# One 512-column product in place of two 256-column products in the down projections of a streaming-encoder block

## The chip, the core and the metric

The kernel runs on one core of one Trainium2 chip. The metric is the device time of one execution in microseconds (us), lower being better. A core has TensorE (in the rows PE for the products and PEld for the loads of their weights), VectorE (DVE), ScalarE (ACT), GpSimd (POOL) and SyncE (SP, which issues the transfers from HBM). SBUF is the on-chip memory; PSUM holds what TensorE writes, in banks of 512 fp32 values for each of 128 partitions.

## What is computed

One layer on 256 tokens of width 2048: a SwiGLU block, a mixer (a causal convolution group beside a gated DeltaNet group), a second SwiGLU block, each with an adaLN modulation that comes from `c`.

```
mods = (silu(c) @ w_ada + b_ada).reshape(B, 9, 2048)
h = modulate(rmsnorm(x, ffn1_norm), mods[:, 0], mods[:, 1])
x = x + 0.5 * mods[:, 2] * ((silu(h @ wg) * (h @ wu)) @ wd)     # wd: 5632 x 2048
h = modulate(rmsnorm(x, mix_norm), mods[:, 3], mods[:, 4])
x = x + mods[:, 5] * (concat(conv_group(h @ w_in), deltanet_group(h @ w_in)) @ w_out)
h = modulate(rmsnorm(x, ffn2_norm), mods[:, 6], mods[:, 7])
x = x + 0.5 * mods[:, 8] * ((silu(h @ wg2) * (h @ wu2)) @ wd2)
out = rmsnorm(x, final_norm)
```

The change is in the two products with `wd` and `wd2`, the down projections.

## The kernel before

Activations lie transposed: features on partitions, the 256 tokens (`T`) along the free dimension. A weight matrix is cut into 128x128 tiles; each is the stationary operand of a product, and the activations stream past it as 256 columns.

**Split products.** A weight in fp32 is split into two fp32r parts: ACT copies it to `hi` (L122), DVE subtracts to get `lo` (L124); one such step handles half a 1 MB load, that is eight tiles. Activations are kept as two parts too, side by side in one tile `act` of shape [128, 2, 256]: part 0 is the high part `rhi`, part 1 the low part `rlo`. A tile's product is three fp32r products into the same 256 columns of a bank (`mm3`, L151 to L153): whi by rhi, whi by rlo, wlo by rhi. Three buffers each for `hi` and `lo` and four for the raw loads limit how far ACT, DVE and the loads run ahead.

**The stages.** In `ffn` the 44 inner tiles (5632 rows) are taken in two halves of 22 (`FH`). For a half, the up and gate projections come first (`col_pair`, L368; activations are split by L298 and L299), then the down projection: for each of 16 output tiles `m`, 22 tiles of `wd` against the 22 `act` tiles, accumulated in one bank, after which DVE's `residual` (L315) adds gate times bank to x. So there are four stretches of down projection, called here the first, second (block one), third and fourth (block two), of 352 tiles each. In the second and fourth, each x tile is then squared for the next norm (L186 on ACT, L182 on DVE), and in the second also made into the mixer's input (`h_pre`, L264 to L268).

**Beside it.** In block one DVE also reduces the modulation weights `w_ada` in the background (`ada`, L218, 2.3 us each with its own 1 MB load), at a fixed number per weight step. In the mixer DVE runs 240 convolution taps (L552), GpSimd runs the small chains of inverse square roots (L166 to L169, each started by DVE's L160 and L162), and TensorE carries `w_in`, the DeltaNet products and `w_out`. The output product `w_out` takes the DeltaNet half first (most of it in plain fp32, L906) and the convolution half last; L830 transposes the DeltaNet output for it.

**What sets the order.** A scheduler orders the instructions of each engine with its own estimate of their times, along the priorities of program order. An edit in one stage can thus reorder instructions in later ones. Each engine then runs its list strictly in order.

Of the kernel before, what the change touches and what calls it, by code (L numbers as in the profile page):

```python
# [16 lines left out]
T = 256  # L17
# [4 lines left out]
FH = FT // 2  # L22
# [31 lines left out]
class Body:  # L54
# [93 lines left out]
    def mm3(self, out, whi, wlo, rhs, start, stop):  # L148
        nc = self.nc
        rhi, rlo = rhs  # L150
        nc.tensor.matmul(out, lhsT=whi, rhs=rhi, start=start, stop=False)  # L151
        nc.tensor.matmul(out, lhsT=whi, rhs=rlo, start=False, stop=False)  # L152
        nc.tensor.matmul(out, lhsT=wlo, rhs=rhi, start=False, stop=stop)  # L153

    def rsqrt(self, v, n, tag, pool=None, beside=False):

        nc = self.nc
        y = self.tile(pool or self.small, [P, n], tag + "y")
        t = self.tile(self.small, [P, n], tag + "t")
        nc.vector.tensor_scalar(out=t.bitcast(I32), in0=v.bitcast(I32), scalar1=1, scalar2=None,  # L160
                                op0=ALU.logical_shift_right)
        self.seed = nc.vector.tensor_scalar(out=y.bitcast(I32), in0=t.bitcast(I32), scalar1=-1.0, scalar2=1597463007.0,  # L162
                                            op0=ALU.mult, op1=ALU.add)
        for _ in range(3):
            if beside:
                nc.gpsimd.tensor_tensor(out=t, in0=y, in1=y, op=ALU.mult)  # L166
                nc.gpsimd.tensor_tensor(out=t, in0=t, in1=v, op=ALU.mult)
                nc.gpsimd.tensor_scalar(out=t, in0=t, scalar1=-0.5, scalar2=1.5, op0=ALU.mult, op1=ALU.add)
                nc.gpsimd.tensor_tensor(out=y, in0=y, in1=t, op=ALU.mult)  # L169
                continue  # L170
            nc.vector.scalar_tensor_tensor(out=t, in0=y, scalar=-0.5, in1=y, op0=ALU.mult, op1=ALU.mult)
            nc.vector.tensor_tensor(out=t, in0=t, in1=v, op=ALU.mult)
            nc.vector.scalar_tensor_tensor(out=y, in0=t, scalar=1.5, in1=y, op0=ALU.add, op1=ALU.mult)
        return y
# [152 lines left out]
    def ffn(self, which, gate, done, after):  # L327
        gu, wd, f0 = self.gu_d[which], self.wd_d[which], len(done)
        for half in range(2):
            acts = list(done) if half == 0 else []  # L330
            for f in range(half * FH + len(acts), (half + 1) * FH):
                ps = [self.bank(self.spare if f == f0 else None)[:, 0:T] for _ in range(2)]
                self.col_pair(ps, gu[f - f0])
                acts.append(self.ffn_evac(*ps))
            n = 0
            for ch in range(FH):
                for hi, lo in self.weights(wd[half, ch]):
                    for k in range(8):
                        m, j = divmod(n, FH)
                        if j == 0:  # L340
                            ps = self.bank()
                        self.mm3(ps[:, 0:T], hi[:, k, :], lo[:, k, :], self.rhs(acts[j]), j == 0, j == FH - 1)
                        if j == FH - 1:
                            while not half and self.ready < gate * 16 + m:
                                next(self.bg[0])
                            self.residual(m, ps[:, 0:T], gate)
                            if half:
                                self.squares(m)
                                after(m)
                        n += 1  # L350
# [668 lines left out]
```

## Time and profile before

| | |
|---|---|
| runs | 1944.02 us median of 3 (1943.39 to 1948.23) |
| the profiled execution | 1943.16 us, of which the span of its instructions is 1941.1 us |
| TensorE products busy | 1894.9 us, 98% of the span, 16206 products |
| DVE busy | 1493.6 us, 77% |
| ACT busy | 916.1 us, 47% |
| DMA | 503.63 MB, mean 259 GB/s |

A busy TensorE is not one at its peak, since its products overlap; how fast it goes is read from the distance between the starts of two products.

### The profile page before, as it was taken

The numbers are of one execution on the slowest core, as the hardware profiler recorded it, in microseconds if no ns is written. First come the engines' busy times: TensorE is split into PE (matmuls) and PEld (weight loads), VectorE is DVE, ScalarE is ACT, GpSimd is POOL, SyncE is SP. The second block draws the span as 40 slices with busy tenths as digits, with TensorE's granted clock in tenths as the row PEclk, the third lists the DMA queues.
The fourth block names the chain that finished last, engine by engine and source line by source line (L and its number), as shares of the span: only waits on it lengthen the run. The fifth ranks groups of instructions, "written<-read, shape, count | busy, mean of one in ns | idle before, by whom it ended". The sixth has DMA issues, their size and how long they took to land.

```text
span 1941.1 us, 38412 instructions
## 1 busy us (share of the span) xinstructions
PE 1894.9 (98%) x16206; PEld 1873.8 (97%) x16206; DVE 1493.6 (77%) x2191; ACT 916.1 (47%) x1298; POOL 96.8 (5%) x195
## 2 busy tenths in 40 slices
PE   5999999999999999999999899999999999999997
PEld 4999999999999999999999889999999999999997
DVE  6989898888878899889999888867775455555554
ACT  3454553344444445754546436544443344444453
POOL 1000000000000000070022300000000000000000
PEclk9999999999999999999999999999999999999999
DMA  8998788899989897457664265567776555555552
GB/s 322 388 361 357 266 338 337 347 349 349 359 350 361 325 350 312 176 182 273 241 207 153 87 240 196 194 238 280 298 278 213 194 194 195 195 195 196 196 195 87
DMA packets 71087, 503.63 MB, mean 259 GB/s; under 512 B 8321, under 2 KB 8961, under 8 KB 10497
## 3 DMA queue, kind: packets, MB, share of 16 engines
q1 hardware_dynamic: 69554, 499.60, 67.9%
q8 instruction: 127, 2.08, 0.4%
q0 software_dynamic: 1360, 1.58, 0.3%
q14 instruction: 46, 0.38, 0.1%
HBM read 498.52 MB, written 2.62 MB: 258 GB/s over the span
## 4 chain that ended last, share of the span: by engine, by line
PE 89%; DVE 5%; POOL 2%; ACT 2%; DMA 1%; issue 1%; DVEq 0%; SPq 0%; ACTq 0%; POOLq 0%
PE ps L368 36%; PE ps L153 16%; PE ps L152 16%; PE ps L151 16%; PE ps L906 2%; DVE lo L124 1%; DMA raw<-in_wa 1%; PE ps L684 1%; DVE raw L218 1%; DVE cva L552 1%; POOL dt L520 1%; ACT hi L122 1%; DVE kq L246 0%; DMA raw<-in_w_ada 0%; DMA x<-in_x 0%
## 5 line engine op out<-in xcount | busy, mean ns | idle before, releaser
L122 ACT ACTIVATE hi<-raw 128x1024 fp32r<-128x1024 f32 x643 | 681.8, 1061 | 893.0 <-PE ps L152 423.8
L124 DVE TENSOR_TENSOR lo<-raw,hi 128x1024 fp32r<-128x1024 f32 x643 | 786.5, 1225 | 371.0 <-ACT hi L122 369.6
L368 PE MATMUL ps<-h,hi 128*128 128x256 f32 x4160 | 640.7, 276 | 0.0
L368 PEld LDWEIGHTS ps<-h,hi 128*128 128x128 f32 x4160 | 548.9, 188 | 0.0
L152 PE MATMUL ps<-h,hi 128*128 128x256 f32 (+1 forms) x1664 | 459.3, 281 | 3.2 <-DVE h L249 3.2
L151 PE MATMUL ps<-h,hi 128*128 128x256 f32 (+1 forms) x1664 | 454.1, 280 | 7.2 <-ACT hi L122 3.9
L153 PE MATMUL ps<-h,lo 128*128 128x256 f32 (+1 forms) x1664 | 439.8, 280 | 0.3 <-DVE lo L124 0.2
L368 PE MATMUL ps<-h,lo 128*128 128x256 f32 x2080 | 404.8, 276 | 0.0
L151 PE MATMUL ps<-act,hi 128*128 128x256 f32 x1408 | 387.1, 276 | 1.0 <-ACT hi L122 1.0
L152 PE MATMUL ps<-act,hi 128*128 128x256 f32 x1408 | 387.5, 276 | 0.0
L153 PE MATMUL ps<-act,lo 128*128 128x256 f32 x1408 | 386.4, 276 | 0.8 <-DVE lo L124 0.8
L218 DVE CUSTOM_DVE_ANT_0 raw<-raw,cb 128x2048 f32<-128x2048 f32 x144 | 329.5, 2290 | 6.6 <-DMA raw<-in_w_ada 6.3
L151 PEld LDWEIGHTS ps<-h,hi 128*128 128x128 f32 x1664 | 311.4, 189 | 9.2 <-ACT h L248 4.4
L152 PEld LDWEIGHTS ps<-h,hi 128*128 128x128 f32 x1664 | 312.9, 188 | 5.0 <-DVE h L249 3.7
L368 PEld LDWEIGHTS ps<-h,lo 128*128 128x128 f32 x2080 | 313.2, 188 | 0.0
L153 PEld LDWEIGHTS ps<-h,lo 128*128 128x128 f32 x1664 | 302.6, 189 | 2.4 <-DVE lo L124 1.1
L151 PEld LDWEIGHTS ps<-act,hi 128*128 128x128 f32 x1408 | 264.0, 188 | 1.4 <-ACT hi L122 1.4
L153 PEld LDWEIGHTS ps<-act,lo 128*128 128x128 f32 x1408 | 263.3, 188 | 1.2 <-DVE lo L124 1.2
L152 PEld LDWEIGHTS ps<-act,hi 128*128 128x128 f32 x1408 | 264.0, 188 | 0.0
L552 DVE SCALAR_TENSOR_TENSOR cva<-xz,prm,cva 128x251 f32<-128x251 f32 (+15 forms) x240 | 105.3, 483 | 1.2 <-ACT cva L548 0.7
L315 DVE SCALAR_TENSOR_TENSOR x<-ps,mods,x 128x256 f32<-128x256 f32 x96 | 46.2, 482 | 27.1 <-PE ps L153 26.5
L906 PE MATMUL ps<-xz,raw 128*128 128x256 f32 x224 | 50.9, 386 | 0.3 <-DVE x L315 0.3
(238 smaller groups left out, 921.1 us busy)
## 6 DMA issues: line engine op xcount, KB each, us to landing
raw<-in_w_ada SPq DMA_DIRECT2D x144, 1024.0 KB, 6.5
raw<-in_gu SPq DMA_DIRECT2D x130, 1024.0 KB, 4.9
raw<-in_wd SPq DMA_DIRECT2D x88, 1024.0 KB, 4.9
raw<-in_w_in SPq DMA_DIRECT2D x42, 1024.0 KB, 5.0
raw<-in_wa SPq DMA_DIRECT2D x40, 1024.0 KB, 8.5
raw<-in_w_out SPq DMA_DIRECT2D x16, 1024.0 KB, 4.8
raw<-in_wk SPq DMA_DIRECT2D x6, 1024.0 KB, 6.5
raw<-in_gw SPq DMA_DIRECT2D x6, 1024.0 KB, 4.7
```

Of the source, the lines that this page charges most:

```text
L122: nc.scalar.activation(out=hi, in_=raw, func=AF.Copy)
L124: nc.vector.tensor_tensor(out=lo, in0=raw, in1=hi.bitcast(F32), op=ALU.subtract)
L151: nc.tensor.matmul(out, lhsT=whi, rhs=rhi, start=start, stop=False)
L152: nc.tensor.matmul(out, lhsT=whi, rhs=rlo, start=False, stop=False)
L153: nc.tensor.matmul(out, lhsT=wlo, rhs=rhi, start=False, stop=stop)
L218: nc.vector.tensor_tensor_reduce(out=w, in0=w, in1=self.cb, scale=1.0, scalar=0.0, op0=ALU.mult, op1=ALU.add, accum_out=self.macc[:, n:n + 1])
L315: self.nc.vector.scalar_tensor_tensor(out=xm, in0=ps, scalar=self.mods[:, gate * 16 + m:gate * 16 + m + 1], in1=xm, op0=ALU.mult, op1=ALU.add)
L368: nc.tensor.matmul(ps[g], lhsT=w[:, 2 * k + g, :], rhs=r, start=start, stop=stop)
L520: nc.gpsimd.tensor_scalar(out=gs[:, i, :], in0=self.low, scalar1=g2[:, b * 4 + i:b * 4 + i + 1], scalar2=None, op0=ALU.mult)
L552: self.taps[j] = nc.vector.scalar_tensor_tensor(out=acc[:, i:T], in0=xs[:, 0:T - i], scalar=w(TAPS - 1 - i), in1=acc[:, i:T], op0=ALU.mult ...
L684: nc.tensor.matmul(ps[:, i * P:(i + 1) * P], lhsT=lhs[:, i, :], rhs=rhs[:, i, :], start=True, stop=True)
L906: nc.tensor.matmul(ps, lhsT=w[:, k, :], rhs=self.zs[k], start=k == 0, stop=k == 7)
```

## The change

`mm3` gives way to `mm2` in the down projections alone. One product of whi now streams both activation parts, 512 columns, into a whole bank: its first half collects whi by rhi, its second whi by rlo. wlo by rhi, 256 columns, goes on top of the second half. `residual` then adds the two halves of the bank to x one after the other, which is one DVE instruction more for each `m`, 64 in all. TensorE has 1408 products fewer and as many columns as before.

```
+    def mm2(self, bank, whi, wlo, rhs, start, stop):
+
+
+        nc = self.nc
+        nc.tensor.matmul(bank, lhsT=whi, rhs=rhs, start=start, stop=False)
+        nc.tensor.matmul(bank[:, 1, :], lhsT=wlo, rhs=rhs[:, 0, :], start=False, stop=stop)
...
                         if j == 0:
-                            ps = self.bank()
-                        self.mm3(ps[:, 0:T], hi[:, k, :], lo[:, k, :], self.rhs(acts[j]), j == 0, j == FH - 1)
+                            ps = self.bank().rearrange("p (g t) -> p g t", g=2)
+                        self.mm2(ps, hi[:, k, :], lo[:, k, :], acts[j], j == 0, j == FH - 1)
                         if j == FH - 1:
                             while not half and self.ready < gate * 16 + m:
                                 next(self.bg[0])
-                            self.residual(m, ps[:, 0:T], gate)
+                            for g in range(2):
+                                self.residual(m, ps[:, g, :], gate)
```

The lines of everything below the new function move by seven or eight: L315 becomes L322, L218 L225, L552 L560, L160 L167, L162 L169, L207 L214.

TensorE at the end of the fourth stretch, before: three products for each tile of `wd`.

```order
L151 MATMUL ps_22782<-act_21366,hi_22831 128x256
L152 MATMUL ps_22782<-act_21366,hi_22831 128x256
L153 MATMUL ps_22782<-act_21366,lo_22833 128x256
L151 MATMUL ps_22782<-act_21490,hi_22831 128x256
L152 MATMUL ps_22782<-act_21490,hi_22831 128x256
L153 MATMUL ps_22782<-act_21490,lo_22833 128x256
```

The same place in the change, two tiles' products and the sum over tokens that follows:

```order
L159 MATMUL ps_21459<-act_20358,hi_21494 128x512
L160 MATMUL ps_21459<-act_20358,lo_21496 128x256
L159 MATMUL ps_21459<-act_20482,hi_21494 128x512
L160 MATMUL ps_21459<-act_20482,lo_21496 128x256
L202 MATMUL ps_21519<-col,acc_20548 128x1 x2
```

A tile costs two products in place of three; what follows is in the same order.

DVE in the mixer, before, at the DeltaNet's output norm: `rqy` starts the chain of the query norm on GpSimd, and `ot`, which reads what that chain leaves in `osc`, starts the next. Between them stood 17 rows; these are the last of them.

```order
L552 SCALAR_TENSOR_TENSOR cva_11373<-xz_11371,prm,cva_11373 128x255
L124 TENSOR_TENSOR lo_13438<-raw_13434,hi_13436 128x1024
L552 SCALAR_TENSOR_TENSOR cva_11216<-xz_11214,prm,cva_11216 128x254
L218 ISA raw_13680,macc<-raw_13680,cb 128x2048
L218 ISA macc 128x1
L552 SCALAR_TENSOR_TENSOR cva_11373<-xz_11371,prm,cva_11373 128x254
L160 TENSOR_SCALAR ot_12877<-osc_12872 128x8
```

The same place in the change, from `rqy` to `ot`:

```order
L169 TENSOR_SCALAR rqy_12112<-rqt_12113 128x16
L784 SCALAR_TENSOR_TENSOR R_11411<-ps_12244,nbk_9279,R_11411 128x128 x2
L560 SCALAR_TENSOR_TENSOR cva_10233<-xz_10231,prm,cva_10233 128x232
L560 SCALAR_TENSOR_TENSOR cva_10390<-xz_10388,prm,cva_10390 128x232
L124 TENSOR_TENSOR lo_12669<-raw_12637,hi_12667 128x1024
L560 SCALAR_TENSOR_TENSOR cva_10233<-xz_10231,prm,cva_10233 128x231
L560 SCALAR_TENSOR_TENSOR cva_10390<-xz_10388,prm,cva_10390 128x231
L124 TENSOR_TENSOR lo_12705<-raw_12701,hi_12703 128x1024
L560 SCALAR_TENSOR_TENSOR cva_10233<-xz_10231,prm,cva_10233 128x230
L560 SCALAR_TENSOR_TENSOR cva_10390<-xz_10388,prm,cva_10390 128x230
L167 TENSOR_SCALAR ot_12205<-osc_12200 128x8
```

The scheduler has moved `ot` up: it now follows `rqy` after ten instructions, not 17 rows, and the weight remainders (L124) that TensorE needs next stand behind it.

TensorE in the mixer, in the change, around the product that spreads the convolution group's norm over the partitions (L214, before L207). `h_12854` to `h_12871` are the DeltaNet half of `w_out`'s input, `h_12958` is the first tile of the convolution half, which comes out of that norm.

```order
L214 MATMUL ps_12952<-ht_12949,ones 128x256
L153 MATMUL ps_13170<-h_12854,lo_13168 128x256
L151 MATMUL ps_13170<-h_12858,hi_13166 128x256
L152 MATMUL ps_13170<-h_12858,hi_13166 128x256
L153 MATMUL ps_13170<-h_12858,lo_13168 128x256
L151 MATMUL ps_13170<-h_12867,hi_13166 128x256
L152 MATMUL ps_13170<-h_12867,hi_13166 128x256
L153 MATMUL ps_13170<-h_12867,lo_13168 128x256
L151 MATMUL ps_13170<-h_12871,hi_13166 128x256
L152 MATMUL ps_13170<-h_12871,hi_13166 128x256
L153 MATMUL ps_13170<-h_12871,lo_13168 128x256
L151 MATMUL ps_13210<-h_12958,hi_13206 128x256
```

Ten products now stand between the norm's product and the first that needs the normed tile; before it was followed by 13 plain products of L906 and 48 split ones. SP's list is the same row for row.

## Rows read from the trace of the kernel before

**Rows 1.** The page: span, busy engines, the chain that ended last.

```profile
span 1941.1 us, 38412 instructions
...
PE 1894.9 (98%) x16206; PEld 1873.8 (97%) x16206; DVE 1493.6 (77%) x2191; ACT 916.1 (47%) x1298; POOL 96.8 (5%) x195
...
PE 89%; DVE 5%; POOL 2%; ACT 2%; DMA 1%; issue 1%; DVEq 0%; SPq 0%; ACTq 0%; POOLq 0%
```

**Rows 2.** Busy time by stretch: the four down projections in order.

```profile
core 0: us, PE busy (x) PEld busy (x) DVE busy (x) ACT busy (x) POOL busy (x), PEclk, DMA share, GB/s
282.60:404.00 121.40, 119.60 (x1036) 118.72 (x1035) 101.63 (x121) 47.10 (x48) 0.00 (x0) 1.00 0.88 343
644.00:763.00 119.00, 119.00 (x1052) 119.00 (x1051) 109.90 (x159) 59.38 (x91) 0.00 (x0) 1.00 0.90 355
1448.50:1567.50 119.00, 119.00 (x1052) 119.00 (x1052) 63.04 (x65) 46.87 (x46) 0.00 (x0) 1.00 0.57 206
1807.50:1926.50 119.00, 119.00 (x1053) 119.00 (x1052) 63.17 (x73) 57.56 (x74) 0.00 (x0) 1.00 0.45 160
```

**Rows 3.** Timeline of TensorE's products in the third stretch: start, duration, line.

```profile
1500.00 0.28 PE L153 MATMUL ps<-act,lo 128*128 128x256 f32 x1
1500.11 0.28 PE L151 MATMUL ps<-act,hi 128*128 128x256 f32 x1
1500.23 0.28 PE L152 MATMUL ps<-act,hi 128*128 128x256 f32 x1
1500.34 0.28 PE L153 MATMUL ps<-act,lo 128*128 128x256 f32 x1
```

**Rows 4.** Plain fp32 products: two merged timeline rows, and durations (min/median/max ns).

```profile
1130.38 11.82 PE L906 MATMUL ps<-xz,raw 128*128 128x256 f32 x54
...
L906 PE MATMUL ps<-xz,raw x224: 379/379/796, 1104.0 to 1156.1; 128*128 128x256 f32 x112
...
1074.69 0.95 PE L606 MATMUL ps<-ones,ht 128*128 128x1 f32 x8
...
L606 PE MATMUL ps<-ones,ht x64: 164/250/250, 818.6 to 1075.4; 128*128 128x1 f32 x64
```

**Rows 5.** Busy time in a stretch of 258-column split products.

```profile
1212.00:1236.00 24.00, 24.00 (x199) 23.95 (x199) 20.09 (x44) 13.64 (x22) 0.00 (x0) 1.00 0.48 176
```

**Rows 6.** DVE's groups in the second stretch, and two adjacent residual adds.

```profile
L124 DVE TENSOR_TENSOR lo<-raw,hi 128x1024 fp32r<-128x1024 f32 x44 | 53.8, 1223 | 7.3 <-ACT hi L122 7.2
...
L315 DVE SCALAR_TENSOR_TENSOR x<-ps,mods,x 128x256 f32<-128x256 f32 x15 | 7.2, 481 | 1.8 <-PE ps L153 1.8
...
300.08 0.88 DVE L315 SCALAR_TENSOR_TENSOR x<-ps,mods,x 128x256 f32<-128x256 f32 x2 [2.39 <-PE ps L153]
```

**Rows 7.** Waits in the first stretch: total us, times, longest.

```profile
PEld ps L151 <- ACT hi L122: 1.4, 2, 0.8
PEld ps L153 <- DVE lo L124: 1.2, 2, 0.7
```

**Rows 8.** Busy time at the end of the second stretch, with the transfer rate.

```profile
744.00:763.00 19.00, 19.00 (x170) 19.00 (x169) 17.89 (x27) 9.16 (x13) 0.00 (x0) 1.00 0.98 404
```

**Rows 9.** Timeline: the last residual add of the fourth stretch.

```profile
1927.02 0.48 DVE L315 SCALAR_TENSOR_TENSOR x<-ps,mods,x 128x256 f32<-128x256 f32 x1 [5.53 <-PE ps L153]
```

**Rows 10.** Timeline of the mixer's end on DVE, PE and ACT, and the taps' group.

```profile
1079.83 0.18 DVE L162 TENSOR_SCALAR rqy<-rqt 128x16 int32<-128x16 int32 x1
...
1090.60 0.17 DVE L160 TENSOR_SCALAR ot<-osc 128x8 int32<-128x8 int32 x1 [1.23 <-POOL osc L812]
...
L552 DVE SCALAR_TENSOR_TENSOR cva<-xz,prm,cva 128x251 f32<-128x251 f32 (+15 forms) x240 | 105.3, 483 | 1.2 <-ACT cva L548 0.7
...
1101.35 2.71 PE L830 MATMUL ps<-ident,A 128*128 128x128 f32 x8 [5.57 <-ACT A L818]
...
1150.25 0.59 PE L207 MATMUL ps<-ht,ones 128*128 128x256 f32 x2
...
1154.62 0.41 ACT L298 ACTIVATE h<-cva 128x256 fp32r<-128x256 f32 x1
```

## The prediction, made before the changed kernel had run

> **What bounds the kernel now.** I read the page first: TensorE's products cover 98% of the span, and 89% of the chain that ended last is TensorE [rows 1]. But busy says little of products that overlap, so the next view is busy time by stretch, cut at the four down projections [rows 2]. In the second, third and fourth, TensorE is never idle and holds 1052 or 1053 products in 119.0 us, at a granted clock of 1.00, which is 2.4 GHz. Less the one still running at the cut that is 119.0 / 1051 = 0.1132 us from start to start, and single rows of the timeline show the same 0.11 or 0.12 us steps without a gap [rows 3]. These three stretches are bound by how fast TensorE takes one product after another; DVE is busy for 53% of the third and fourth, and 92% of the second [rows 2]. The first stretch is slightly different: 1036 products at 0.1132 us would take 117.3 of its 121.4 us, so 4.1 us go to waits, and these are for the split of weights: 1.4 us for ACT's `hi` and 1.2 us for DVE's `lo` among them [rows 7]. So what the change is worth is the time of one tile of `wd`, three steps of 0.1132, 339.7 ns, times 1408 tiles, less what DVE does to it.
>
> **What a product's 113.2 ns is made of.** 256 columns at 2.4 GHz and one cycle each would be 106.7 ns. The 6.5 ns above that decide this case. The nearest rows are the plain fp32 products. Those of L906, 256 columns each, stand 54 in 11.82 us; less the last one's own 379 ns that is 11.44 / 53 = 215.9 ns from start to start [rows 4], or 512 cycles (213.3 ns) and 2.6. So a product that occupies the array for 512 cycles has a surplus of 2.6 ns, not 13. And products of one single column still take (0.95 - 0.25) / 7 = 0.10 us on average [rows 4], though their column is nothing. Each carries a 128x128 weight load, and I take that load as the floor: with 256 columns the array's 107 to 109 ns are a little shorter than the load behind it, with 512 cycles the load is hidden. A wide fp32r product then takes what L906 takes, 215.9 ns, and the narrow one that follows keeps 113.2, since the next tile's whi is loaded behind it.
>
> **The sum.** A tile costs 215.9 + 113.2 = 329.1 ns in place of 339.7. 10.6 ns by 352 tiles is 3.7 us for each stretch, 14.9 us for four. The bounds of this term: if the 6.5 ns belong to every product whatever its length, the wide one takes 219.8 and a tile gains 6.7 ns, 9.4 us in all; if the narrow product too escapes the floor behind a wide one (109.3), a tile gains 14.5 ns, 20.4 us. If the surplus belongs to the columns, nothing is gained (a rival, below). I take 14.9, because L906 has the cycles of the wide product and the same weight load.
>
> The Trainium skill, page "TensorE: Matmul & The Clock Gate", section "Wait — 56ns, not 53.3ns?", has start to start as N / 2.4 GHz and about 2.5 ns. L906's 215.9 ns agrees with it, the 113.2 ns of the split products do not (it would have 109.2). By the page alone a tile goes from 327.6 to 325.0 ns, an estimate, and the change would give 3.6 us.
>
> **DVE** gets 64 instructions, 16 in each stretch. Two adjacent residual adds take 0.88 us, the second starting 0.40 us after the first [rows 6], so 6.4 us more DVE work in each stretch. In the third and fourth DVE has 63 of 119 us of work, and the second add hides in that room; without that cover it would be 0.40 us a time, 6.4 us a stretch. The bank it holds longer is one of four, each filled for 22 tiles (7.2 us), so TensorE does not wait for it.
>
> In the second stretch there is little room: 109.9 + 6.4 = 116.3 us of work against 352 x 0.3291 = 115.8 us of TensorE. DVE also waits there 7.2 us for ACT's `hi` and 1.8 us for residuals [rows 6]. Behind a waiting residual stand the next `lo` remainders, which TensorE needs. The loss lies between 0 (DVE's lead of up to two weight steps covers the 0.5 us it lacks, and the waits for `hi` shrink as DVE falls behind) and 116.3 + 9.0 - 115.8 = 9.5 us (every wait stays). I take 1.5, near the low end, as a late engine no longer waits.
>
> In the first stretch DVE has 101.6 + 6.4 = 108.0 us of work for 117.7 us, enough on average. At its start, where the split is what TensorE waits for [rows 7], one more residual goes ahead of the next remainder, 0.4 us, and the following ones a little later: 1.0 us, between 0 and 6.4.
>
> **Transfers.** SP's list is unchanged. The first two stretches move 343 and 355 GB/s [rows 2]; 3% faster they ask for 353 and 366, and 404 GB/s are reached in the last 19 us of the second [rows 8]. I cost it at nothing.
>
> **The end.** The last residual starts at 1927.02 us with nothing behind it but the norm and the store [rows 9]; a second add there costs its 0.4 us in full.
>
> **The mixer** is not edited, but its order is. Before, TensorE waited 5.57 us for the DeltaNet output (L830) [rows 10]. In the changed order the query-norm chain is started earlier against TensorE's work and the first head group's chain runs alone on GpSimd, so most of this wait should go: up to 5.6 us gained. Two things give it back. `ot` waits for GpSimd's `osc`, which takes 1090.60 - 1080.01 = 10.6 us after `rqy` [rows 10]; in between DVE now has two remainders at 1.22, six taps at 105.3 / 240 = 0.44 and two short adds, some 5.5 us in all, so it stands still for about 5 us with the next remainder behind it, and TensorE, about two steps (5.4 us) of weights ahead, then loses perhaps 2 to 3. And the convolution norm's product now has ten products (1.1 us) between it and the first that needs the normed tile; before, that tile's high part ended 1155.0 - 1150.25 = 4.8 us after the product [rows 10]. So about 3 us of wait appear there. These cancel; I count zero, and from a gain of 5.6 to a loss of 6 for the range.
>
> Together: -14.9 + 1.5 + 1.0 + 0.4 + 0 = -12.0 us. The profiled execution took 1943.2 us (its span and 2.1 us around it), 0.9 us below the median of the runs shown; from 1943.2 I get 1931.2, and as a median 1932.
>
> **The rivals.**
>
> *The columns set the pace.* The change has as many columns as before. If the split products' 6.5 ns come with the columns (a stream slowed by 6%), the wide product takes 2 x 113.2 = 226.4 ns, a tile 339.6, and nothing is gained; DVE's 2.9 us remain: 1944.0 + 2.9 = 1947, no change. For it: the two kinds of product differ only in type, and only the split ones show the 6.5 ns. Against it: the 0.10 us of one-column products. By the rule of the Trainium skill's page above, an estimate again, 3.6 us less 2.9 would be gained, 1943, which is no change either.
>
> *DVE and the mixer take the gain.* If in the second stretch half of the 9.5 us is lost and the mixer loses 4, the sum is -14.9 + 4.8 + 1.0 + 0.4 + 4 = -4.7: 1939, no change. For it: 92% busy DVE in strict order. Against it: block two alone, with DVE half idle, gives 7.5.
>
> *The wide stream meets the weight loads* and ends on the other side. Split products with 258 columns, whose parts lie two columns further in their tiles, start 199 in 24.0 us, 24.0 / 198 = 121.2 ns apart [rows 5], 8 ns more than 256 columns for two more, so the place in SBUF from which a stream is read can cost time. The wide product reads part 0 and part 1 in one stream. If it is slowed as these are over its whole length, it takes 242 ns and a tile 242.4 + 121.2 = 363.6, 23.9 ns more than now: 1408 x 0.0239 = 33.7 us, 1944 + 33.7 + 2.9 = 1981. It decides from a tile above 339.7 - 2.0 + 4.1 = 342 ns, a wide product of 229. Against it: the tiles do not move, and the parts already are read from these places at 113.2.
>
> *Both escape the floor*: 325.2 ns a tile, -20.4 + 2.9 = -17.5, 1926.
>
> **The numbers.** The forecast 0.59, both escape 0.10, columns 0.12, DVE and mixer 0.11, wide stream slower 0.08. I hold 0.3% (5.8 us) to be about what a measurement of this kernel tells from no change. Faster: 0.59 + 0.10 and 0.01 of the DVE case, 0.70; same 0.22; slower 0.08. The range runs from 1923 (20.4 gained, nothing lost) to 1943 (the mixer's loss of 6 and the low end of the pair, 9.4, with DVE at 3); it leaves out the slow stream and most of the columns' case.
>
> **What the profile would show.** Wide products 216 ns before the next start and narrow ones 113, four stretches of 116 us (the first 119 to 120), 1408 products fewer. Wrong: a wide product of 220 or more; TensorE waiting for `lo` in the second stretch by more than 2 us; the wait at L830 still there, or waits around the convolution norm beyond 6 us.

## The result: slower by 1.1%, in the products that were to gain

The changed kernel takes 1969.08 us (median of 4, 1965.71 to 1973.51), the kernel before 1946.12 us beside it (median of 4, 1943.39 to 1954.66). The ratio is 1.0112, with a 95% interval of 1.0073 to 1.015. The forecast was 1932, with a range up to 1943: wrong in sign, since the wide product takes 229 or 236 ns where 215.9 had been put in.

The page of the changed kernel, against [rows 1]: fewer products, and yet more time of TensorE.

```profile
span 1967.1 us, 35638 instructions
...
PE 1913.7 (97%) x14798; PEld 1826.4 (93%) x14798; DVE 1519.2 (77%) x2255; ACT 918.4 (47%) x1301; POOL 107.9 (5%) x195
...
PE 88%; DVE 5%; DMA 3%; POOL 2%; issue 1%; ACT 1%; SPq 0%; DVEq 0%; ACTq 0%; POOLq 0%
```

Busy time by stretch, the four down projections, against [rows 2] (same columns):

```profile
283.80:410.40 126.60, 124.27 (x705) 107.12 (x704) 109.35 (x141) 48.50 (x51) 0.00 (x0) 1.00 0.87 337
649.80:772.80 123.00, 123.00 (x705) 107.33 (x705) 115.17 (x173) 59.71 (x91) 0.00 (x0) 1.00 0.90 344
1464.10:1588.00 123.90, 123.90 (x705) 107.03 (x704) 70.01 (x80) 47.23 (x46) 0.00 (x0) 1.00 0.57 198
1827.60:1951.60 124.00, 124.00 (x705) 107.16 (x705) 70.01 (x88) 57.80 (x74) 0.00 (x0) 1.00 0.44 153
```

The reader is to see three things. TensorE is busy without a hole in the last three stretches, so nothing that it waits for explains them. The granted clock is 1.00 as before. And the last two stretches, in which DVE has over 50 us to spare, are the longest: 704 products in 123.9 us are 352 ns for a pair, against the 339.7 of three narrow products and the 329.1 of the forecast. The second add did double its work in the second stretch (L322, 30 adds, against 15 in [rows 6]), and DVE found the room:

```profile
L322 DVE SCALAR_TENSOR_TENSOR x<-ps,mods,x 128x256 f32<-128x256 f32 x30 | 14.4, 480 | 2.2 <-PE ps L160 2.2
```

The timeline of TensorE in the fourth stretch, against [rows 3]: start, duration, line.

```profile
1859.87 0.40 PE L159 MATMUL ps<-act,hi 128*128 128x512 f32 x1
1860.10 0.28 PE L160 MATMUL ps<-act,lo 128*128 128x256 f32 x1
1860.22 0.40 PE L159 MATMUL ps<-act,hi 128*128 128x512 f32 x1
1860.45 0.28 PE L160 MATMUL ps<-act,lo 128*128 128x256 f32 x1
1860.57 0.40 PE L159 MATMUL ps<-act,hi 128*128 128x512 f32 x1
```

Two pairs in 0.70 us, 350 ns each at this resolution. The trace holds the starts in ns, and most pairs fall into two kinds: 229 ns for the wide product, or 236, each with 117 or 118 for the narrow one, so about 347 or 353 ns a tile. One kind holds for many tiles on end: in the third and fourth stretches nearly all tiles of the first two banks take 347, those of the other fourteen 353.

Where the 26.0 us between the two profiled spans lie, from the first to the last start of each stretch: the four stretches themselves 3.0, 3.4, 4.4 and 4.4 us, together 15.2; the way from the second to the third (the mixer and block two's first up projection; the up projections between the other stretches take 239.5 us in both) 6.3; the time before the first stretch 3.3; the tail 1.0. The 3.3 are not the change's: TensorE's list is the same row for row up to there, and over the sixteen profiles of this case the first down product starts between 277.4 and 282.5 us.

### The profile page after: what moved, and what is told of

It reads as the page before. It is cut to its first block, busy times and chain, and to the rows that moved or that the text cites. A ratio compares the mean times of both kernels' runs of the same rounds, so it can differ in the third digit from the quotient of the medians.

```text
span 1967.1 us, 35638 instructions
## 1 busy us (share of the span) xinstructions
PE 1913.7 (97%) x14798; PEld 1826.4 (93%) x14798; DVE 1519.2 (77%) x2255; ACT 918.4 (47%) x1301; POOL 107.9 (5%) x195
## 4 chain that ended last, share of the span: by engine, by line
PE 88%; DVE 5%; DMA 3%; POOL 2%; issue 1%; ACT 1%; SPq 0%; DVEq 0%; ACTq 0%; POOLq 0%
PE ps L376 36%; PE ps L159 16%; PE ps L160 8%; PE ps L153 8%; PE ps L152 8%; PE ps L151 8%; PE ps L914 2%; DMA raw<-in_w_ada 2%; DVE lo L124 1%; DVE cva L560 1%; PE ps L692 1%; DVE raw L225 1%; DMA raw<-in_wa 0%; DMA ls<-scr_l 0%; DVE kq L253 0%
## 5 line engine op out<-in xcount | busy, mean ns | idle before, releaser
L124 DVE TENSOR_TENSOR lo<-raw,hi 128x1024 fp32r<-128x1024 f32 x643 | 786.0, 1224 | 352.3 <-ACT hi L122 351.4
L159 PE MATMUL ps<-act,hi 128*128 128x512 f32 x1408 | 492.6, 395 | 0.8 <-ACT hi L122 0.8
L160 PE MATMUL ps<-act,lo 128*128 128x256 f32 x1408 | 387.4, 279 | 1.6 <-DVE lo L124 1.6
L225 DVE CUSTOM_DVE_ANT_0 raw<-raw,cb 128x2048 f32<-128x2048 f32 x144 | 329.0, 2286 | 8.8 <-DMA raw<-in_w_ada 8.6
L159 PEld LDWEIGHTS ps<-act,hi 128*128 128x128 f32 x1408 | 261.6, 187 | 63.2 <-ACT hi L122 1.4
L160 PEld LDWEIGHTS ps<-act,lo 128*128 128x128 f32 x1408 | 263.7, 187 | 5.6 <-DVE lo L124 2.8
L560 DVE SCALAR_TENSOR_TENSOR cva<-xz,prm,cva 128x251 f32<-128x251 f32 (+21 forms) x240 | 105.3, 480 | 6.0 <-DMA ls<-scr_l 5.6
L322 DVE SCALAR_TENSOR_TENSOR x<-ps,mods,x 128x256 f32<-128x256 f32 x160 | 76.7, 481 | 38.1 <-PE ps L160 29.3
L914 PEld LDWEIGHTS ps<-xz,raw 128*128 128x128 f32 x224 | 42.3, 190 | 6.4 <-DVE xz L842 0.8
```

The lines of the kernel that those rows point to most:

```text
L124: nc.vector.tensor_tensor(out=lo, in0=raw, in1=hi.bitcast(F32), op=ALU.subtract)
L159: nc.tensor.matmul(bank, lhsT=whi, rhs=rhs, start=start, stop=False)
L160: nc.tensor.matmul(bank[:, 1, :], lhsT=wlo, rhs=rhs[:, 0, :], start=False, stop=stop)
L225: nc.vector.tensor_tensor_reduce(out=w, in0=w, in1=self.cb, scale=1.0, scalar=0.0, op0=ALU.mult, op1=ALU.add, accum_out=self.macc[:, n:n + 1])
L322: self.nc.vector.scalar_tensor_tensor(out=xm, in0=ps, scalar=self.mods[:, gate * 16 + m:gate * 16 + m + 1], in1=xm, op0=ALU.mult, op1=ALU.add)
L560: self.taps[j] = nc.vector.scalar_tensor_tensor(out=acc[:, i:T], in0=xs[:, 0:T - i], scalar=w(TAPS - 1 - i), in1=acc[:, i:T], op0=ALU.mult ...
```

## The experiments

All edits are to the changed kernel. Except for `halves3` and `oneadd`, each version ran once, so what counts there is the distance between starts, not the total time.

**Is it the place in SBUF?** Three kernels move the `act` tiles by 64, 128 and 192 bytes, counted within 256; a pad of `ACT % 256` bytes stands ahead of their pool. The line of 256 bytes in the expectations is the unit in which this pad counts; no run shows that SBUF has such lines.

```
-ACT = 192
+ACT = 0        # act0; 64 in act64, 128 in act128
```

> The changed kernel with one constant altered: the act tiles, which the down projections stream, start 64 bytes into a 256-byte line of SBUF instead of 0, which is where the lo weights start. Place theory (the stream's place against the hi and lo weight loads sets how far it is slowed): the wide product moves by 6 ns or more from its 229 or 236, to 216 at best or 242 and more at worst, and the third stretch of 123.96 us with it (115.9 to 127). Rival, pace of the product itself: wide stays 229 or 236, narrow 117 to 118, third stretch 123.9 to 124.0.

> The same with act tiles 128 bytes into a line, away from hi (192) and lo (64) alike. Place theory: if any place frees the wide product it is this one or the present one; a tile of 329 to 340 ns, third stretch 116 to 119.6 us. Rival, pace of the product itself: no change, 347 to 354 ns a tile, 123.9 to 124.0 us.

> The same with act tiles 192 bytes into a line, which is where the hi weights start. Place theory: the worst place for the product of hi, a wide of 242 ns or more, third stretch 126 us or more. Rival, pace of the product itself: no change, 347 to 354 ns a tile, 123.9 to 124.0 us.

Measured, third stretch, mean of wide and narrow: act0 232.8 and 119.2, act64 233.2 and 119.9, act128 233.0 and 116.9, against 234.8 and 117.7 in the change. The stretch takes 123.78, 124.19 and 123.07 us, against 123.96. The place changes the pattern (in act64 nearly every pair is 233 or 234 and 120) and moves a tile by 3 ns at most; none comes near 340. The supposed worst place, that of `hi`, was the best of the four. For places within 256 bytes the theory falls.

**Is it the accumulator?** The narrow product adds into the half that was written longer ago:

```
-        nc.tensor.matmul(bank[:, 1, :], lhsT=wlo, rhs=rhs[:, 0, :], ...)
+        nc.tensor.matmul(bank[:, 0, :], lhsT=wlo, rhs=rhs[:, 0, :], ...)
```

> The changed kernel with the narrow product (wlo by rhi) added into the first half of the bank, where the wide product wrote 256 columns earlier, instead of the second half, which it has only just written; the sum is the same. Theory of the accumulator (a product that adds to columns just written waits for them): narrow falls from 117.6 to 113.2, a tile by 4 ns, third stretch 122.4 us or less. Rival, pace of the products themselves: nothing moves, 123.9 to 124.0 us.

Measured: stretches of 122.99, 123.96 and 123.96 us, the changed kernel's to the hundredth; narrow 117 or 118. It falls too.

**DVE and the mixer apart from the products.** Two kernels take the change apart. `halves3` has everything but the wide product:

```
-        nc.tensor.matmul(bank, lhsT=whi, rhs=rhs, start=start, stop=False)
+        nc.tensor.matmul(bank[:, 0, :], lhsT=whi, rhs=rhs[:, 0, :], start=start, stop=False)
+        nc.tensor.matmul(bank[:, 1, :], lhsT=whi, rhs=rhs[:, 1, :], start=False, stop=False)
```

> Everything of the change but the wide product: whi by rhi into the first half of the bank, whi by rlo and wlo by rhi into the second, three products of 256 columns, and both residual adds. DVE, ACT and GpSimd stand in the mixer in the changed kernel's order. If the wide product's pace costs the down projections their 15 us and the second adds cost only the mixer's order and the tail: three starts of 113.2, stretches of 119.6 us, 691 us from the second stretch to the third, 1945 + 6 + 1 = 1952. Rival, the second adds hold the stretches up: 123 to 124 us each, 1965 or more.

Measured: 1955.3 us (median of 10) against 1949.83 (of 13), ratio 1.0028 (1.0016 to 1.0039). Busy time in its second stretch, for comparison with [rows 2]:

```profile
646.50:765.50 119.00, 119.00 (x1053) 119.00 (x1052) 114.10 (x171) 59.59 (x91) 0.00 (x0) 1.00 0.91 354
```

1053 products in 119.0 us, as before the change, with DVE at 114.1 us of work. The three later stretches take 119.57 us each, to the hundredth the time before. So the second adds cost the stretches nothing (0.5 us in the first); their 5.5 us lie outside the stretches. In the profile the way from the second stretch to the third is 9.9 us longer than before the change and the tail 1.0, but that is one profile against one.

`oneadd` has the wide product and only the first of the two adds:

```
-                            for g in range(2):
+                            for g in range(1):
```

> The changed kernel with only the first of the two residual adds; the second half of the bank (whi by rlo and wlo by rhi) is left out of x. GpSimd's list is then that of the kernel before, row for row. If the pace of the wide product is the cost: 347 or 354 ns a tile still, stretches of 123 to 124 us, 685 us from the second to the third as before, 1945 + 15 = 1960. Rival, the adds: a tile of 340 ns or less and 1945 or less.

Measured: 1964.01 us (median of 4), ratio 1.0072 (1.005 to 1.0093), so 14.0 us. Its stretches take 1.7, 3.4, 4.4 and 4.4 us more than before the change, 13.9 together; pairs are 347 or 353. With DVE's share taken away the loss in the stretches is whole. Within their intervals the parts add up: 14.0 (9.8 to 18.1) and 5.5 (3.1 to 7.6) are 19.5 of the 21.8 us that the ratio 1.0112 stands for. From the second to the third stretch it needs 688.6 us, 3.6 more than in the profile before although GpSimd's list is the same. There the pace differs: from start to start, split products of 256 columns that follow one another within 0.2 us take 115.08 ns in the mean against 114.27, which over 4187 steps is 3.4 us; 30% of them take over 115 ns against 16%, more of the slower rhythm that the last section shows. This need not come from the edit: in the twelve profiles whose TensorE list on this way is the changed kernel's row for row, the same mean lies between 114.31 and 115.04.

**The wide product alone**, without wlo by rhi:

```
-        nc.tensor.matmul(bank, lhsT=whi, rhs=rhs, start=start, stop=False)
-        nc.tensor.matmul(bank[:, 1, :], lhsT=wlo, rhs=rhs[:, 0, :], start=False, stop=stop)
+        nc.tensor.matmul(bank, lhsT=whi, rhs=rhs, start=start, stop=stop)
```

> The changed kernel without wlo by rhi, so one 512-column product a tile and half the weight loads; what wlo by rhi adds is left out. Prediction's theory (weight load as a floor under short products): 216 ns from start to start. Rival, the columns set the pace: 226.4, twice 113.2. Rival, the turn from a wide to a narrow product costs, and wide ones alone don't pay it: 216 to 222, with the 229 or 236 gone. The stretches may be held by the weights' split, so the most frequent distance is what counts.

A merged row of the third stretch's timeline, 20 wide products:

```profile
1479.64 4.74 PE L159 MATMUL ps<-act,hi 128*128 128x512 f32 x20
```

Less the last one's own 0.39 that is 4.35 / 19 = 229 ns from start to start. The starts are 226, 229 and 232 in turn, mean 228.9. This is neither the 216 of the floor theory nor free of the surplus when there is no turn to a narrow product; it is 2.5 above the 226.4 of the pace by columns.

**Other widths.** Between the first and the last tile of a bank, block two's products are cut short: wide ones in the third stretch, three narrow ones in the fourth.

```
+        if wide:
+            nc.tensor.matmul(flat[:, 0:wide], lhsT=whi, rhs=r[:, 0:wide], ...)
+        else:
+            nc.tensor.matmul(flat[:, 0:w], lhsT=whi, rhs=r[:, 0:w], ...)
+            nc.tensor.matmul(flat[:, T:T + w], lhsT=whi, rhs=r[:, T:T + w], ...)
+        nc.tensor.matmul(flat[:, T:T + w], lhsT=wlo, rhs=r[:, 0:w], ...)
```

> Block two with other widths (columns left out, except in the first and last of a bank's 22 tiles): third stretch, the wide product cut to 384, 448, 496 and 512 columns for four output tiles each, the narrow one 256; fourth stretch, three products of 256, then 224, 192 and 128 columns. Prediction's theory, a floor of about 113 ns under each product: narrow ones stay at 100 to 113 at 224 and 192, and a wide one of 496 takes 216 or less. Rival, pace by columns: 113.2 / 256 = 0.442 ns a column, 99 at 224, 85 at 192, and a wide one 7 ns shorter for each 16 columns. Rival, a fixed loss at the turn between widths: the wide one stays 13 to 20 ns above its columns at every width.

Timeline rows: 384 columns, then three products of 128.

```profile
1467.94 0.33 PE L166 MATMUL ps<-act,hi 128*128 128x384 f32 x1
1468.11 0.28 PE L170 MATMUL ps<-act,lo 128*128 128x256 f32 x1
1468.22 0.34 PE L166 MATMUL ps<-act,hi 128*128 128x384 f32 x1
1468.40 0.28 PE L170 MATMUL ps<-act,lo 128*128 128x256 f32 x1
...
1924.80 0.28 PE L168 MATMUL ps<-act,hi 128*128 128x128 f32 x1
1924.91 0.27 PE L169 MATMUL ps<-act,hi 128*128 128x128 f32 x1
1925.03 0.27 PE L170 MATMUL ps<-act,lo 128*128 128x128 f32 x1
1925.13 0.27 PE L168 MATMUL ps<-act,hi 128*128 128x128 f32 x1
```

Three products of 128 columns in 0.33 us: half the columns, the same distance. The mean over all is 110.7 ns at 128, 111.3 at 192 and 111.5 at 224 columns. So there is a floor of about 111 ns, but it lies 2 ns below the 113.2 of 256 columns, not at it. Wide products take 173, 205, 229 and 236 ns (medians) for 384, 448, 496 and 512 columns. That is 13, 18, 22 and 23 ns above their columns at 2.4 GHz (160, 186.7, 206.7, 213.3): a surplus that grows with the columns, not a fixed one. Expected had been 99 and 85 ns at 224 and 192 by one theory and 216 at 496 by the other; each was right on one half.

Unlooked for: the three products of 256 columns in the first four banks take about 356 ns a tile in three banks and 340 in one, though the same three take 339.7 throughout `halves3`. What differs is a wide product at each end of a bank.

**Traffic beside TensorE, and the weight load.** Third stretch: the weights of the first load serve all tiles. Fourth: 64 weight columns for each product.

```
...
+                    if ch == 0:
+                        kept = list(self.weights(wd[half, ch]))
+                    steps = kept
...
+        mm(bank[0:64], lhsT=whi[:, 0:64], rhs=rhs, start=start, stop=False)
+        mm(bank[0:64, 1, :], lhsT=wlo[:, 0:64], rhs=rhs[:, 0, :], start=False, stop=stop)
```

> Block two with two stretches altered, the rest as changed. Third stretch: every tile uses the weights of the first load, so there is no transfer, copy or subtraction beside TensorE once it runs (the sums are other ones). Fourth stretch: only 64 of the 128 weight columns are loaded for each product, so half of each output tile is left out. Theory that other engines' and the transfers' traffic in SBUF slows the stream: third stretch, wide 216 to 222, narrow 109 to 112; fourth as before, 229 or 236. Theory that the load of the next weights slows the stream: third as before, 347 to 354 ns a tile; fourth, wide 216 to 222. Theory that an fp32r stream has this pace by itself: both stay, 229 to 236.

Busy time in the third stretch, and two rows each of the third's and the fourth's timeline:

```profile
1500.00:1560.00 60.00, 60.00 (x347) 52.84 (x347) 7.74 (x16) 0.00 (x0) 0.00 (x0) 1.00 0.00 1
...
1519.94 0.39 PE L159 MATMUL ps<-act,hi 128*128 128x512 f32 x1
1520.17 0.28 PE L160 MATMUL ps<-act,lo 128*128 128x256 f32 x1
...
1879.96 0.28 PE L171 MATMUL ps<-act,lo 128*64 128x256 f32 x1
1880.08 0.40 PE L170 MATMUL ps<-act,hi 128*64 128x512 f32 x1
```

With ACT at nothing, DVE at 7.7 of 60 us and 1 GB/s of transfers, 347 products in 60 us are still 347 ns a pair: here the first bank runs mostly with the 236 and all later ones with the 229, but none comes lower. With half the weight columns (128*64) the means are 233.8 and 118.5. Neither the other engines' traffic nor the size of the load makes the pace.

**The same columns twice, and two wide products.** Third stretch: part 0 is streamed twice, part 1 not at all. Fourth: wlo meets both parts as well.

```
+        mm(bank, lhsT=whi, rhs=rhs[:, 0:1, :].to_broadcast([P, 2, T]), start=start, stop=False)
...
+        mm(bank, lhsT=whi, rhs=rhs, start=start, stop=False)
+        mm(bank, lhsT=wlo, rhs=rhs, start=False, stop=stop)
```

> Block two with two stretches altered. Third: the wide product streams part 0 twice, so the same 256 columns in place of parts 0 and 1 (rlo is left out). Fourth: wlo too meets both parts in a wide product, two of 512 columns a tile (a term more than the reference has). Place theory: third stretch, wide falls below 226 as part 1 is not read; fourth stays at 229 to 236 for both. Theory of the turn between widths: third stays, fourth, with no turn, 226 to 229 for both as in the run without the narrow product. Pace by the columns: third 229 to 236, fourth 226 to 232.

Third stretch: 234.8 and 117.7 ns, 123.96 us, as in the change; part 1 has no share in it. Fourth: 233.2 and 229.0 ns in the mean, so 1024 columns in 462 ns, 0.451 a column, with no narrow product between.

**Order and entry.** Third stretch: wide, wide, narrow, narrow over two tiles. Fourth: three narrow products for every tile but the first.

```
+        mm(bank, lhsT=hi[:, k, :], rhs=acts[j], start=j == 0, stop=False)
+        if k % 2:
+            for q in (1, 0):
+                mm(bank[:, 1, :], lhsT=lo[:, k - q, :], rhs=acts[j - q][:, 0, :], ...)
```

> Block two with two stretches altered, sums as in the reference. Third: the order over two tiles is wide, wide, narrow, narrow, half as many turns from one width to the other. Fourth: three products of 256 columns for every tile but the first, which is one wide and one narrow product. Theory of two gaits (a product of another width throws the stream out of the fast gait of 0.442 ns a column, and it stays out): fourth, 117 to 120 ns for all or most of the three products, a stretch of 123 to 125.5 us though 351 of 352 tiles are as in the kernel before; third, 347 to 354 ns a tile. Rival, the turn costs each time: fourth 113.2 ns and 119.6 us as in the run of the two halves; third, about half of the 7 to 14 ns by which a tile is longer, 340 to 347 ns, 119.7 to 122 us.

Third: 233.1 and 118.3 ns in the mean, 123.56 us; half the turns don't halve the loss, so it isn't a price of the turn. Fourth, timeline rows from the first bank and from the tenth:

```profile
1835.81 0.28 PE L164 MATMUL ps<-act,hi 128*128 128x256 f32 x1
...
1836.52 0.28 PE L164 MATMUL ps<-act,hi 128*128 128x256 f32 x1
...
1899.96 0.28 PE L164 MATMUL ps<-act,hi 128*128 128x256 f32 x1
...
1900.30 0.28 PE L164 MATMUL ps<-act,hi 128*128 128x256 f32 x1
```

In the first bank two tiles take 0.71 us (118 ns a product), later one takes 0.34 (113). After the one wide product nearly all narrow ones of the first bank's 22 tiles run at 117 to 124 ns, those from the second bank on at 113 or 114; the stretch takes 119.91 us. So there are two rhythms for the same products, as expected, but a wide product at the start doesn't hold them in the slower one for the stretch: half of that expectation falls.

**The type.** First a mixture: bf16 wide products (the upper two bytes of the fp32r values) with fp32r narrow ones, and in the fourth stretch three narrow fp32r products without traffic.

```
+        w = whi.bitcast(B).rearrange("p (m t) -> p t m", t=2)[:, 1, :]
+        r = rhs.bitcast(B).rearrange("p g (m t) -> p t g m", t=2)[:, 1, :, :]
+        mm(bank, lhsT=w, rhs=r, start=start, stop=False)
+        mm(bank[:, 1, :], lhsT=wlo, rhs=rhs[:, 0, :], start=False, stop=stop)
```

> Block two with two stretches altered. Third: the wide product reads only the upper two bytes of each weight and activation, as bf16 (its sum is less exact), the narrow one stays fp32r. Fourth: three products of 256 columns, as in the kernel before but into two halves, with the weights of the first load throughout, so no transfer, copy or subtraction beside them (the sums are other ones). Pace of the fp32r stream itself: bf16 wide 213 to 219, narrow 113 to 118; fourth 113.2 still. Traffic in SBUF: bf16 wide no better than 226; fourth falls to 109 to 112. The floor of 111.5 by the weight load alone: fourth 111 to 113.2, and not below.

It tells little of the type: a tile takes 363 ns (127.35 us for the stretch) and the starts come in bursts, a narrow product 0.32 us before the next wide one and that 0.04 before the next narrow. To alternate the types costs more than either. The fourth stretch takes 125.10 us, mostly 118 to 124 ns a product without any traffic beside them: the slower rhythm again, in a stretch whose banks begin and end with a wide product. Expected had been 113.2 or less.

Then bf16 for both products, third stretch with columns side by side (a bf16 copy of one `act` tile), fourth with columns 4 bytes apart:

```
+        r = rhs.bitcast(B).rearrange("p g (m t) -> p t g m", t=2)[:, 1, :, :] if strided else rhs
+        mm(bank, lhsT=u, rhs=r, start=False, stop=False)
+        mm(bank[:, 1, :], lhsT=v, rhs=r[:, 0, :], start=False, stop=False)
```

> Block two with two stretches altered; the first and last of a bank's 22 tiles stay as in the change. Both products of the other tiles are bf16 against bf16 (the upper two bytes of the weights). Third stretch: they all stream one bf16 copy of the first act tile, 2 bytes a column side by side (the sums are other ones). Fourth: they stream the upper two bytes of the act tiles, 4 bytes apart (less exact sums). If the pace of 0.44 to 0.46 ns a column is that of fp32r streams: a wide product of 213 to 219 and a narrow one of 107 to 113, a tile of 320 to 332 ns in both, stretches of 113 to 117 us. If it is the pace of any product that alternates with another width: 347 to 354 ns a tile, 122 to 124 us. If it hangs on 4-byte columns in SBUF: the third 320 to 332, the fourth 347 to 354.

Timeline rows of the third stretch (L166 reads `fg`, the copy), then of the fourth:

```profile
1519.74 0.38 PE L166 MATMUL ps<-fg,hi 128*128 128x512 bf16 x1
1519.95 0.27 PE L167 MATMUL ps<-fg,lo 128*128 128x256 bf16 x1
1520.06 0.38 PE L166 MATMUL ps<-fg,hi 128*128 128x512 bf16 x1
...
1521.04 0.38 PE L166 MATMUL ps<-fg,hi 128*128 128x512 bf16 x1
...
1859.82 0.39 PE L166 MATMUL ps<-act,hi 128*128 128x512 bf16 x1
...
1861.18 0.39 PE L166 MATMUL ps<-act,hi 128*128 128x512 bf16 x1
```

Four tiles in 1.30 us, 325 ns each, with the columns side by side; four in 1.36, 340 each, with 4 bytes from column to column. The steps are 216 and 109 in the one, in the mean 226.7 and 114.1 in the other. The 216 also clears PSUM: these products too write and add 512 columns into a whole bank. As one tile was streamed in the third and 22 in the fourth, a control streams one and the same tile in both stretches, the third in bf16 with 4 bytes between columns, the fourth in fp32r:

```
+                        if which == 1 and 0 < j < FH - 1:
+                            (self.mm2r if half else self.bf)(ps, hi[:, k, :], lo[:, k, :], acts[0])
```

> The control of the last run but one: between the first and last of a bank's 22 tiles every product of a stretch in block two streams one and the same act tile (the sums are other ones). Third stretch: bf16 with columns 4 bytes apart. Fourth: fp32r, as in the change. If the distance of the columns in SBUF made the difference of the two bf16 stretches (325 against 340 ns a tile): third 226 and 113 to 114, 340 ns a tile, fourth 229 to 236 and 117 to 118. If it was that one tile was streamed over and over: third 216 and 109, 325 ns a tile, and the fourth below 347.

```profile
1519.75 0.39 PE L166 MATMUL ps<-act,hi 128*128 128x512 bf16 x1
...
1521.11 0.39 PE L166 MATMUL ps<-act,hi 128*128 128x512 bf16 x1
...
1860.13 0.40 PE L171 MATMUL ps<-act,hi 128*128 128x512 f32 x1
...
1861.19 0.40 PE L171 MATMUL ps<-act,hi 128*128 128x512 f32 x1
```

Four tiles in 1.36 us (340 ns) and three in 1.06 (353): 226.7 and 114.1 in the mean for bf16 at 4 bytes, mostly 236 and 117 or 118 for fp32r. So it is not the one tile, it is the distance of the columns that makes 340 of 325, and fp32r adds 7 to 13 more. (The copy in `fg` also lies at another place than `act`; four places of `act` moved an fp32r tile by 3 ns at most.) (In these stretches the first and last tile of each bank are still fp32r.)

## Why the prediction was wrong

**The step that failed** is the one that says what a product's 113.2 ns is made of: "I take that load as the floor", and from it "A wide fp32r product then takes what L906 takes, 215.9 ns, and the narrow one that follows keeps 113.2". Measured are 229 or 236 and 117 or 118, a pair of 347 or 353 in place of 329.1; the term of -14.9 us came out as +15.2 in the profile.

- *The floor.* It exists (about 111 ns for 128 to 224 columns in fp32r; whether the weight load makes it was not tested at these widths) but does not explain 113.2: an fp32r product of 256 columns is a little longer than its floor, so nothing was hidden there that a longer stream could give back. The 0.10 us of the one-column products showed that there is a floor, not that the 256-column product sits on it.
- *L906 as the nearest row.* It has the time of 512 cycles, but only 256 columns. The prediction overlooked that its rows are not whole products: the kernel issues 112 products at L906 (7 x 2 x 8) and the trace holds 224 rows of them [rows 4], so each product left two rows of 215.9 ns (and each one-column product of L606 two as well, 32 in 64 rows). If a row streams its 256 columns once, it takes a new 4-byte column only every 0.84 ns (215.9 / 256), where the wide fp32r product wants one every 0.42 (213.3 / 512), and that could be why it shows no surplus; if it streams them twice, it takes them as fast as the wide product and this reason falls. No run tells which. What the runs share is this: streams with 4 bytes from column to column, fp32r or bf16, run at 0.441 to 0.461 ns a column, the bf16 one side by side at 0.422 (216 / 512).
- *The rule that was put aside.* The Trainium skill, page "TensorE: Matmul & The Clock Gate", section "Wait — 56ns, not 53.3ns?", gives N / 2.4 GHz and about 2.5 ns, by an estimate from it 215.8 for 512 columns and 109.2 for 256. The runs agree with it for bf16 columns side by side (216 and 109) and for no fp32r or bf16 stream with 4 bytes from column to column. L906's rows, which the prediction found to agree with it, fit only if their 256 columns are counted twice. The Trainium skill, page "SBUF — State Buffer", section "Door 1: The DMA port swizzle (why `[64,N]` ≈ `[32,N]`)", has SBUF read in lines of 16 bytes, with a price for each step to a new line and bf16 free up to a stride of 8; here a stride of 2 already costs 10 ns for 512 columns (226 against 216), so on that the measurement decides.

**The rivals.** "The columns set the pace" had the mechanism for the most part: the surplus goes with the columns. It expected 339.6 ns a tile, what three narrow products take, and that is what the bf16 stream at 4 bytes takes; it missed the 7 to 13 ns more that fp32r products of two widths lose. "The wide stream meets the weight loads" had the sign and set its turning point at 342 ns a tile, but its mechanism, the place of the stream, is excluded by the four places, by the same columns streamed twice and by the halved load. "DVE and the mixer take the gain" named a real loss, of 5.5 us, with no gain to take.

**DVE.** 1.5 us in the second stretch and 1.0 in the first were put in; `halves3` shows 0 and 0.5. The late engine does wait less, as argued, and this is read from `halves3`, where TensorE keeps the pace of before: in the second stretch DVE stands still 3.2 us for `hi` and 1.7 before the adds, against 7.2 and 1.8 [rows 6], and TensorE waits for no `lo`.

```profile
L124 DVE TENSOR_TENSOR lo<-raw,hi 128x1024 fp32r<-128x1024 f32 x43 | 52.6, 1223 | 3.2 <-ACT hi L122 3.2
...
L323 DVE SCALAR_TENSOR_TENSOR x<-ps,mods,x 128x256 f32<-128x256 f32 x30 | 14.5, 482 | 1.7 <-PE ps L161 1.6
```

At the tail the last two adds take 1.00 us in place of 0.48 [rows 9], 0.5 more where 0.4 was put; the tail as a whole lost 1.0.

```profile
1951.93 1.00 DVE L322 SCALAR_TENSOR_TENSOR x<-ps,mods,x 128x256 f32<-128x256 f32 x2 [4.85 <-PE ps L160]
```

**The mixer** was counted as zero, from a gain of 5.6 to a loss of 6; it lost 6.3 in the profile (5.5 with the tail by the timed runs of `halves3`). One profile is a thin base for this figure: in the twelve with the changed kernel's TensorE list row for row, this way takes 690.1 to 698.4 us, in part because the waits for `lo` add up to anything from 2.4 to 8.6 us (3.3 in the change). TensorE's waits in the mixer's second part: for whom, total us, times, longest.

```profile
PE ps L153 <- DVE lo L124: 3.0, 2, 2.2
PE ps L151 <- ACT hi L122: 2.2, 1, 2.2
PE ps L151 <- ACT h L305: 2.1, 1, 2.1
PE ps L152 <- DVE h L306: 1.2, 1, 1.2
PE ps L638 <- DVE L L642: 0.9, 1, 0.9
PE ps L735 <- POOL jk L733: 0.8, 1, 0.8
```

The 5.57 us at L830 [rows 10], now L838, are gone from this list, as forecast. The convolution norm's wait is there, 2.1 and 1.2, where about 3 was put. A step of weights comes late by 2.2 us, where 2 to 3 was put, but on another engine: not DVE stands behind the norm's chain but ACT, whose scaling waits for GpSimd's `oy`, with the next `hi` queued behind it (timeline of ACT):

```profile
1105.95 2.46 ACT L826 ACTIVATE A<-A,oy 128x128 f32<-128x128 f32 x8 [5.52 <-POOL oy L824]
...
1108.90 1.04 ACT L122 ACTIVATE hi<-raw 128x1024 fp32r<-128x1024 f32 x1
```

So the three that were seen cancel to within a microsecond (-5.6 and +5.5). What was not seen are the 3.0 us for `lo`, 2.2 of them at one place, the wait of 0.8 at L735, and many small ones: steps of over 0.2 us between two split products of 256 columns are 108 against 61, and what they take beyond the usual pace is, all waits for these products included, 14.1 us more than before, while the other steps take 7.6 less. `halves3` and `oneadd`, one with nearly the changed order and one with GpSimd's old one, show that the 64 adds alone reorder the mixer; the old order keeps its wait at L838 (5.5 us in `oneadd`).

**What stays open.** Why fp32r products of two widths take 229 or 236 and not the 226 of bf16 at the same distance, and what makes the stream go over from one rhythm to the other. Place within 256 bytes, part 1, traffic, size of the load, accumulator and order of the products are excluded as the cause of the loss, though place and traffic shift which rhythm is met. The change of rhythm is no chance event: in the second stretch, the change and the seven versions that edit block two alone, eight profiles in all, have their 14 lasting changes (at least five tiles on both sides) at the same 14 tiles, and each of these is the first or second tile of a bank or of a weight step. What happens there to change the pace is not shown. No version here that forms the full sum beats the kernel before: three narrow products at 113.2 ns are the fastest way found here to stream these columns in fp32r.

## What to carry to other kernels

A surplus over the ideal time of a product is not yet a fixed price per product; before products are merged to save it, find a row in which the same type streams more columns in one product, or measure one. A row of another type with the same time is no substitute, since the trace does not show how it streams its columns, and rows are to be counted against the products in the code. And an edit that gives one engine 64 small instructions can cost in a stage that it doesn't touch, if a scheduler places that stage by its own estimate of time; this is to be priced apart from the edit itself, by a kernel that has only those instructions.

## What was not expected of the hardware

The same instructions run in two rhythms, with no wait between them and the clock at 1.00. In the changed kernel's mixer, an unedited place, split products of 256 columns stand 18 starts in 2.14 us ahead of a wait for `lo`, 118.9 ns apart, and 9 in 1.02 us behind it, 113.3 apart (timeline of TensorE):

```profile
901.78 0.28 PE L153 MATMUL ps<-h,lo 128*128 128x256 f32 x1
...
903.92 0.28 PE L153 MATMUL ps<-h,lo 128*128 128x256 f32 x1
...
906.81 0.28 PE L151 MATMUL ps<-h,hi 128*128 128x256 f32 x1
...
907.83 0.28 PE L151 MATMUL ps<-h,hi 128*128 128x256 f32 x1
```

In the trace before, the mixer's split products of 256 columns likewise take mostly 117 or 118 ns from 800 us, behind the first 258-column products, with three spells of 113 between 830 and 850 us. A wait of 1.8 us at 858 us does not end this: they still take 117 or 118 up to 866 us, and then mostly 113 up to 990, with no wait at the change. A distance read from one place, as the 113.2 here, is thus one of two values that the same products can take.
